# Merge in pieces, 512-column products, two sums by adding transfers and a rotary exchange on ScalarE in a decoder layer

## The chip, the cores and the metric

One core of one Trainium2 chip. TensorE (PE in the profile) multiplies, VectorE (DVE) and ScalarE (ACT) work on its results, GpSimd (POOL) and SyncE (SP) mostly issue transfers. The metric is the device time of one execution in microseconds; shorter is better.

## The reference

One layer of a hybrid decoder trunk, float32, 512 tokens, width 2048. A normalized input goes through one wide projection whose columns feed three attention branches and three gates; the branches are projected back, gated, summed, and projected once more.

```python
h = rms_norm(x, norm_in_g[layer])
proj = jnp.einsum('bsd,de->bse', h, w_in[layer])
(qa, ka, va, za, qb, kb, vb, zb, qm, zm, gates) = jnp.split(proj, split_points, axis=-1)
...
ya = moba_attention(qa, ka, va).reshape(B, S, W_A) * jax.nn.silu(za)
...
g_a, g_b, g_m = jnp.split(jax.nn.sigmoid(gates), N_BRANCH, axis=-1)
merged = (g_a * jnp.einsum('bse,ed->bsd', ya, w_proj_a[layer])
          + g_b * jnp.einsum('bse,ed->bsd', yb, w_proj_b[layer])
          + g_m * jnp.einsum('bse,ed->bsd', ym, w_proj_m[layer]))
x = x + jnp.einsum('bsd,de->bse', merged, w_out[layer])
return rms_norm(x, norm_final_g)
```

`qa`, `ka`, `qb` and `kb` are turned by rotary angles: with a head's 128 channels cut into halves x1 and x2, the result is x1 cos - x2 sin and x2 cos + x1 sin.

## The kernel before

Every float32 operand is split into a high part `hi` (a copy by ACT in the type fp32r) and a remainder `lo` (a difference by DVE), and a product is three products: hi x hi, hi x lo and lo x hi.

The wide projection is done in 65 *pairs* of output units of 128 channels (class `Pair`). Each pair is a 2 x 2 block product in seven block products instead of eight (a Strassen form): sums of weight quarters meet prepared forms of the activations, B11, T1, T2, B21, T3, B22 and T4, each 1024 x 256. B11, T4, B21 and B22 lie in the tiles `kept`, T1, T2 and T3 in tiles called `T`; each tile holds the high and the low part. One of the seven is `seven()`: for eight blocks of 128 rows it issues L397 (hi weights, high form), L398 (hi weights, low form) and L399 (lo weights, high form), 256 columns each, so a pair has 168 products. Three accumulators x, y and z in PSUM take them.

The weights of a pair come as quarters of 128 x 1024 (512 KB) by `quarter` (L378, on SP's queue): a11, a21, s (which is a22), a12, and a22 once more. They use 18 buffers `raw`, of which the forms T1 to T3 hold 12. `parts_1024` (L387 on ACT, L388 on DVE) splits one into `whi` and `wlo`, three buffers each. In the order of the seven products the split weights are p1 = a11; p5 = s after L435 (s = a21 + s); p6 = s after L441 (s = s + a11); p2 = a12; q7 = a21 after L448 (a21 = a21 + a11); q3 = s after L454 (s = s + a12); and p4 = a22. ACT copies x or y out at L443, L450 and L456; DVE forms the results g1 and g2 at L462, L468 and L474 from PSUM and these copies; ACT writes the last quarter, with sign and activation, at L481. L470 and L476 apply an activation (37 pairs have one for g2).

`Pair.run` emits a pair in seven steps, and after each it emits a share of a list `later` of small jobs, so that DVE's and ACT's side work lies among PE's products. The last step of a pair begins the next one (`follower`). The order on each engine is made by the planner of the Tile framework, from its own costs and what is ready; it is not the order of the text, so that L435 of the next pair, for example, stands ahead of L468 of this one. Each engine then works through its queue in order.

Turning (`rotate`): t1 = g cos, t2 = the exchanged halves of g times sin, L506 and L509, each on 64 partitions, then a sum; 40 times.

The last part before the output projection is the merge stage: eight times three pairs of gates (24 pairs). After each pair L1101 multiplies both results with the branch's projection `pj`, fetched from DRAM on POOL's queue, and L1103 adds them to `merged`; after three pairs `merged_forms` makes the activation forms for the output projection (five operations on DVE, L921 to L924 and the remainder of L927, one on ACT) and stores three tiles in DRAM (`waiting`). Then the output projection runs (L1038 to L1040), with final normalization.

Small tiles of 128 x 512 share 25 slots (`slot`). The code that the diff touches:

## Time and profile before

| what | value |
|---|---|
| three runs | 1997.02, 1999.28 and 2000.56 us, median 1999.28 us |
| the profiled execution | 2003.55 us, of which its span is 2001.8 us |
| PE, DVE, ACT, POOL busy | 98%, 76%, 51%, 6% of the span |
| matrix products, vector operations, activations | 14225, 1948, 1567 |
| bytes moved | 318.90 MB, 159 GB/s on average |
| loads of w_in of 512 KB | 331 issues |

The span runs from the first to the last instruction of one profiled execution. An engine's share is the time in which it had an instruction at work; a product of PE is longer in the profile than its distance to the next one, since products overlap, so products are told by distance here. Of a stage, the rows of a stretch tell more than the shares of the whole.

### The profile page before, as it was taken

What the parts mean: (1) busy time and instruction counts of PE and PEld (TensorE: products, weight loads), DVE (VectorE), ACT (ScalarE), POOL (GpSimd) and SP (SyncE); (2) the same over time, 40 slices, a digit from 0 to 9 for tenths busy, and PEclk for the clock granted to TensorE, in tenths of its full rate; (3) what the DMA queues carried; (4) which work ended last, traced back from release to release, by engine and by line L of the source; (5) the groups of instructions that cost most, each with busy time, mean ns of one, the idle gap of its engine ahead of it and who ended that gap; (6) DMA issues with size and microseconds to landing.
All of it is one profiled execution on the core that took longest, in us unless ns stands there. A gap on an engine that the chain in (4) does not pass through costs nothing.

```text
span 2001.8 us, 34970 instructions
## 1 busy us (share of the span) xinstructions
PE 1962.3 (98%) x14225; PEld 1850.3 (92%) x14225; DVE 1527.3 (76%) x1948; ACT 1019.9 (51%) x1567; POOL 118.4 (6%) x226
## 2 busy tenths in 40 slices
PE   8999999999999999999999999999999999999998
PEld 6889999789999999889999999989999999998776
DVE  5976777249999888348888889646878878778887
ACT  7654565245656665235545464644444444445445
POOL 0000010010000000010000000012000000001010
PEclk9999999999999999999999999999999999999999
DMA  9565444333333434433443434356445444558654
GB/s 364 189 222 172 149 159 156 134 112 132 127 122 126 128 118 157 142 132 117 122 138 106 134 115 127 117 174 205 140 163 181 161 155 143 180 171 302 251 181 152
DMA packets 100993, 318.90 MB, mean 159 GB/s; under 512 B 17376, under 2 KB 20320, under 8 KB 100832
## 3 DMA queue, kind: packets, MB, share of 16 engines
q1 hardware_dynamic: 84624, 264.21, 39.5%
q0 software_dynamic: 16064, 52.44, 7.7%
q8 instruction: 111, 1.82, 0.4%
q14 instruction: 50, 0.41, 0.1%
q10 hardware_dynamic: 144, 0.02, 0.0%
HBM read 285.13 MB, written 31.49 MB: 158 GB/s over the span
## 4 chain that ended last, share of the span: by engine, by line
PE 86%; DVE 5%; DMA 5%; issue 2%; ACT 1%; SPq 0%; ACTq 0%; DVEq 0%; POOL 0%; POOLq 0%
PE acc L397 19%; PE acc L398 19%; PE acc L399 19%; PE acc L112 5%; PE acc L110 5%; PE acc L111 5%; DMA raw<-in_w_in 2%; PE acc L1039 2%; PE acc L1040 2%; PE acc L1038 2%; DVE wlo L388 1%; DMA rows<-in_x 1%; PE att L162 1%; PE att L161 1%; PE att L163 1%
## 5 line engine op out<-in xcount | busy, mean ns | idle before, releaser
L387 ACT ACTIVATE whi<-raw 128x1024 fp32r<-128x1024 f32 x507 | 537.1, 1060 | 605.7 <-PE acc L398 359.6
L388 DVE TENSOR_TENSOR wlo<-raw,whi 128x1024 fp32r<-128x1024 f32 x507 | 617.7, 1220 | 137.5 <-ACT whi L387 125.8
L397 PE MATMUL acc<-kept,whi 128*128 128x256 f32 x2080 | 590.0, 284 | 13.7 <-DVE g L468 13.7
L398 PE MATMUL acc<-kept,whi 128*128 128x256 f32 x2080 | 586.8, 282 | 0.0
L399 PE MATMUL acc<-kept,wlo 128*128 128x256 f32 x2080 | 586.3, 282 | 0.0
L397 PE MATMUL acc<-T,whi 128*128 128x256 f32 x1560 | 441.6, 283 | 0.5 <-ACT ha L443 0.5
L399 PE MATMUL acc<-T,wlo 128*128 128x256 f32 x1560 | 441.0, 283 | 0.0
L398 PE MATMUL acc<-T,whi 128*128 128x256 f32 x1560 | 440.9, 283 | 0.0
L397 PEld LDWEIGHTS acc<-kept,whi 128*128 128x128 f32 x2080 | 394.3, 190 | 15.6 <-issue 14.7
L398 PEld LDWEIGHTS acc<-kept,whi 128*128 128x128 f32 x2080 | 394.7, 190 | 0.4
L399 PEld LDWEIGHTS acc<-kept,wlo 128*128 128x128 f32 x2080 | 394.8, 190 | 0.0
L397 PEld LDWEIGHTS acc<-T,whi 128*128 128x128 f32 x1560 | 297.8, 191 | 1.1 <-ACT ha L443 0.7
L399 PEld LDWEIGHTS acc<-T,wlo 128*128 128x128 f32 x1560 | 298.1, 191 | 0.4 <-DVE wlo L388 0.4
L398 PEld LDWEIGHTS acc<-T,whi 128*128 128x128 f32 x1560 | 298.2, 191 | 0.3
L91 DVE TENSOR_TENSOR wlo<-raw,whi 128x1024 fp32r<-128x1024 f32 x78 | 94.9, 1222 | 128.6 <-ACT whi L90 128.5
L90 ACT ACTIVATE whi<-raw 128x1024 fp32r<-128x1024 f32 x78 | 82.2, 1059 | 158.9 <-PE acc L111 105.7
L435 DVE TENSOR_TENSOR raw<-raw 128x1024 f32<-128x1024 f32 x65 | 79.5, 1223 | 89.9 <-DMA raw<-in_w_in 87.8
L110 PE MATMUL acc<-shi,whi 128*128 128x512 f32 x320 | 126.6, 396 | 0.5 <-ACT pr L145 0.5
L111 PE MATMUL acc<-slo,whi 128*128 128x512 f32 x320 | 126.5, 395 | 0.0
L112 PE MATMUL acc<-shi,wlo 128*128 128x512 f32 x320 | 126.4, 395 | 0.0
L441 DVE TENSOR_TENSOR raw<-raw 128x1024 f32<-128x1024 f32 x65 | 79.3, 1221 | 1.0
L454 DVE TENSOR_TENSOR raw<-raw 128x1024 f32<-128x1024 f32 x65 | 79.3, 1220 | 0.9
(268 smaller groups left out, 2585.3 us busy)
## 6 DMA issues: line engine op xcount, KB each, us to landing
raw<-in_w_in SPq DMA_DIRECT2D x331, 512.0 KB, 3.8
raw<-in_w_out SPq DMA_DIRECT2D x48, 512.0 KB, 6.6
raw<-in_w_mem SPq DMA_DIRECT2D x32, 512.0 KB, 5.2
projected<-pr POOLq DMA_DIRECT2D x48, 256.0 KB, 2.5
pj<-projected POOLq DMA_DIRECT2D x48, 256.0 KB, 5.6
raw<-in_w_pm SPq DMA_DIRECT2D x16, 512.0 KB, 3.8
raw<-in_w_pa SPq DMA_DIRECT2D x16, 512.0 KB, 4.2
mg<-waiting SPq DMA_DIRECT2D x9, 512.0 KB, 8.4
```

Of the source, the lines that this page charges most:

```text
L90: nc.scalar.activation(hi, raw, AF.Copy)
L91: nc.vector.tensor_tensor(lo, raw, hi.bitcast(F32), op=OP.subtract)
L110: nc.tensor.matmul(ps, whi, hi[i], start=i == 0, stop=False)
L111: nc.tensor.matmul(ps, whi, lo[i], start=False, stop=False)
L112: nc.tensor.matmul(ps, wlo, hi[i], start=False, stop=i == n - 1)
L387: nc.scalar.activation(hi, raw, AF.Copy)
L388: nc.vector.tensor_tensor(lo, raw, hi.bitcast(F32), op=OP.subtract)
L397: nc.tensor.matmul(ps, hi[:, sl], f[0], start=start and k == 0, stop=False, skip_group_check=True)
L398: nc.tensor.matmul(ps, hi[:, sl], f[1], start=False, stop=False, skip_group_check=True)
L399: nc.tensor.matmul(ps, lo[:, sl], f[0], start=False, stop=stop and k == 7, skip_group_check=True)
L435: nc.vector.tensor_tensor(s, a21, s, op=OP.add)
L441: nc.vector.tensor_tensor(s, s, a11, op=OP.add)
```

## The change

- `seven` issues two products per block instead of three: the hi weights meet the high and the low part of a form in one instruction of 512 columns, in two strips of 256 (the forms are views of both parts now), and the lo weights meet the high part, 256 columns, into the first half. The accumulators are 512 wide.
- The copies and sums out of PSUM are 512 wide (`both_tile`, three buffers), and `joined` adds the two halves of each on DVE. The last quarter is copied by ACT with its sign, added by DVE, and gets its activation apart.
- For pairs outside the memory branch (`adding`, 60 of 65) the sums L448 and L454 are made by transfers on POOL's queue that read the quarter a11 or a12 from DRAM again and add it to a21 or s in the buffer.
- `rotate` lets ACT copy the exchanged halves into t2, and DVE multiplies t2 by sin in one operation of 128 partitions. The table's signs are exchanged.
- The merge after each gate pair, and `merged_forms`, now cut into two, go into `later` and run beside the next pair, but for the last triple.
- `ones`, `diag`, `v` and the half tiles come from the slots; `v3` and `p` share a tag.

```diff
 
-    ones = sb.tile([P, P], F32, name="ones")
+    ones = slot("ones")[:, :P]
     nc.gpsimd.memset(ones, 1.0)
...
             for t in range(n):
-                diag = sb.tile([P, P], F32, name="diag", bufs=1)
+                diag = slot("diag")[:, :P]
                 nc.vector.tensor_scalar(diag, ident, col[:, t:t + 1], None, op0=OP.mult)
...
         b11, b12, b21, b22 = g0[:, :256], g0[:, 256:], g1[:, :256], g1[:, 256:]
-        u, v = slot("u"), sb.tile([P, 256], F32, name="halft", tag="halft", bufs=4)
+        u, v = slot("u"), slot("v")[:, :256]
         nc.vector.tensor_tensor(u[:, :256], b11, b12, op=OP.subtract)
...
         t = wide_tile("T12", F32R)
-        two = split(u, (t[:, :512], t[:, 512:]))
-        T["T1"].append([p[:, :256] for p in two])
-        T["T2"].append([p[:, 256:] for p in two])
+        split(u, (t[:, :512], t[:, 512:]))
+        two = t.rearrange("p (a c) -> p a c", a=2)
+        T["T1"].append(two[:, :, :256])
+        T["T2"].append(two[:, :, 256:])
         if k % 2 == 0:
...
         t = T["store"][:, k % 2 * 512:(k % 2 + 1) * 512]
-        T["T3"].append(split(v, (t[:, :256], t[:, 256:])))
+        split(v, (t[:, :256], t[:, 256:]))
+        T["T3"].append(t.rearrange("p (a c) -> p a c", a=2))
         split(g0, kept[k])
...
 
-    T["B11"] = [(t[:, 0, :256], t[:, 1, :256]) for t in held[:8]]
-    T["T4"] = [(t[:, 0, 256:], t[:, 1, 256:]) for t in held[:8]]
-    T["B21"] = [(t[:, 0, :256], t[:, 1, :256]) for t in held[8:]]
-    T["B22"] = [(t[:, 0, 256:], t[:, 1, 256:]) for t in held[8:]]
+    T["B11"] = [t[:, :, :256] for t in held[:8]]
+    T["T4"] = [t[:, :, 256:] for t in held[:8]]
+    T["B21"] = [t[:, :, :256] for t in held[8:]]
+    T["B22"] = [t[:, :, 256:] for t in held[8:]]
 
...
 
+    def add_quarter(t, u, half):
+        nc.gpsimd.dma_start(t, w_in[u][:, half * 1024:(half + 1) * 1024], accum_op=OP.add)
+    def both_tile(name):
+        return sb.tile([P, 512], F32, name=name, tag="both", bufs=3)
     def half_tile(name):
-        return sb.tile([P, 256], F32, name=name, tag="halft", bufs=4)
+        return slot(name)[:, :256]
+    def joined(out, t):
+        nc.vector.tensor_tensor(out, t[:, :256], t[:, 256:], op=OP.add)
 
...
 
         hi, lo = parts
...
             f = T[form][k]
-            nc.tensor.matmul(ps, hi[:, sl], f[0], start=start and k == 0, stop=False, skip_group_check=True)
-            nc.tensor.matmul(ps, hi[:, sl], f[1], start=False, stop=False, skip_group_check=True)
-            nc.tensor.matmul(ps, lo[:, sl], f[0], start=False, stop=stop and k == 7, skip_group_check=True)
+            nc.tensor.matmul(ps, hi[:, sl], f, start=start and k == 0, stop=False, skip_group_check=True)
+            nc.tensor.matmul(ps[:, :256], lo[:, sl], f[:, 0, :], start=False, stop=stop and k == 7,
+                             skip_group_check=True)
 
...
         def __init__(self, u1, u2, f1=AF.Copy, f2=AF.Copy):
+            self.adding = u1 < U_QM or u1 >= U_G
             self.units, self.f1, self.f2 = (u1, u2), f1, f2
...
             a12 = quarter(u1, 1)
             p5 = parts_1024(s)
-            x = acc_bank()[:, :256]
+            x = acc_bank()
             seven(x, p1, "B11", start=True)
             nc.vector.tensor_tensor(s, s, a11, op=OP.add)
-            a = half_tile("ha")
+            a = both_tile("ha")
             nc.scalar.copy(a, x)
             yield 1
             p6 = parts_1024(s)
-            y = acc_bank()[:, :256]
+            y = acc_bank()
             seven(y, p5, "T1", start=True)
-            nc.vector.tensor_tensor(a21, a21, a11, op=OP.add)
-            d = half_tile("hd")
+            if self.adding:
+                add_quarter(a21, u1, 0)
+            else:
+                nc.vector.tensor_tensor(a21, a21, a11, op=OP.add)
+            d = both_tile("hd")
             nc.scalar.copy(d, y)
             yield 2
             p2 = parts_1024(a12)
             seven(x, p6, "T2")
-            nc.vector.tensor_tensor(s, s, a12, op=OP.add)
-            b = half_tile("hb")
+            if self.adding:
+                add_quarter(s, u1, 1)
+            else:
+                nc.vector.tensor_tensor(s, s, a12, op=OP.add)
+            b = both_tile("hb")
             nc.scalar.copy(b, x)
             yield 3
             q7 = parts_1024(a21)
-            z = acc_bank()[:, :256]
+            z = acc_bank()
             seven(z, p2, "B21", start=True, stop=True)
             g1 = self.g1 = slot("g1")
-            nc.vector.tensor_tensor(g1[:, :256], z, a, op=OP.add)
+            nc.vector.tensor_tensor(a, z, a, op=OP.add)
+            joined(g1[:, :256], a)
             yield 4
             q3 = parts_1024(s)
...
             seven(x, q7, "T3")
             g2 = self.g2 = slot("g2")
-            nc.vector.scalar_tensor_tensor(g2[:, 256:], x, -1.0, d, op0=OP.mult, op1=OP.subtract)
+            nc.vector.scalar_tensor_tensor(d, x, -1.0, d, op0=OP.mult, op1=OP.subtract)
+            joined(g2[:, 256:], d)
             if self.f2 != AF.Copy:
                 nc.scalar.activation(g2[:, 256:], g2[:, 256:], self.f2)
...
             p4 = parts_1024(a22)
             seven(y, q3, "B22", stop=True)
-            nc.vector.tensor_tensor(g1[:, 256:], y, b, op=OP.add)
+            nc.vector.tensor_tensor(b, y, b, op=OP.add)
+            joined(g1[:, 256:], b)
             if self.f1 != AF.Copy:
                 nc.scalar.activation(g1, g1, self.f1)
...
                 self.follower.begin()
             seven(x, p4, "T4", stop=True)
-            nc.scalar.activation(g2[:, :256], x, self.f2, scale=-1.0)
+            e = both_tile("he")[:, :256]
+            nc.scalar.activation(e, x[:, 256:], AF.Copy, scale=-1.0)
+            nc.vector.scalar_tensor_tensor(g2[:, :256], x[:, :256], -1.0, e, op0=OP.mult, op1=OP.add)
+            if self.f2 != AF.Copy:
+                nc.scalar.activation(g2[:, :256], g2[:, :256], self.f2)
             yield 7
 
...
         def first():
+            nc.scalar.copy(t2[0:64], g[64:128])
+            nc.scalar.copy(t2[64:128], g[0:64])
             nc.vector.tensor_tensor(t1, g, cos, op=OP.mult)
-            nc.vector.tensor_tensor(t2[0:64], g[64:128], sin[64:128], op=OP.mult)
 
         def second():
-            nc.vector.tensor_tensor(t2[64:128], g[0:64], sin[0:64], op=OP.mult)
+            nc.vector.tensor_tensor(t2, t2, sin, op=OP.mult)
             r = t1
...
     M = {f: [None] * 8 for f in ("T1", "T2", "T3")}
-    M.update({f: T[f] for f in ("B11", "T4", "B21", "B22")})
+    M.update({f: [(t[:, 0], t[:, 1]) for t in T[f]] for f in ("B11", "T4", "B21", "B22")})
     waiting = dram.tile([NK, P, 512], F32, name="waiting")
...
     def merged_forms(k):
         g0, g1 = merged[k], merged[8 + k]
...
         u, v = slot("u"), half_tile("v")
-        nc.vector.tensor_tensor(u[:, :256], b11, b12, op=OP.subtract)
-        nc.vector.tensor_tensor(v, b22, b12, op=OP.subtract)
-        nc.vector.scalar_tensor_tensor(u[:, 256:], u[:, :256], -1.0, b22, op0=OP.mult, op1=OP.subtract)
-        nc.vector.scalar_tensor_tensor(b12, u[:, 256:], -1.0, b21, op0=OP.mult, op1=OP.subtract)
-        for at, t in ((waiting[k], g0), (waiting[8 + k], g1), (waiting3[k // 4][:, k % 4 * 256:(k % 4 + 1) * 256], v)):
-            nc.gpsimd.dma_start(at, t)
-        two = split(u)
-        M["T1"][k] = [p[:, :256] for p in two]
-        M["T2"][k] = [p[:, 256:] for p in two]
+        def first():
+            nc.vector.tensor_tensor(u[:, :256], b11, b12, op=OP.subtract)
+            nc.vector.scalar_tensor_tensor(u[:, 256:], u[:, :256], -1.0, b22, op0=OP.mult, op1=OP.subtract)
+            two = split(u)
+            M["T1"][k] = [p[:, :256] for p in two]
+            M["T2"][k] = [p[:, 256:] for p in two]
+        def second():
+            nc.vector.tensor_tensor(v, b22, b12, op=OP.subtract)
+            nc.vector.scalar_tensor_tensor(b12, u[:, 256:], -1.0, b21, op0=OP.mult, op1=OP.subtract)
+            for at, t in ((waiting[k], g0), (waiting[8 + k], g1),
+                          (waiting3[k // 4][:, k % 4 * 256:(k % 4 + 1) * 256], v)):
+                nc.gpsimd.dma_start(at, t)
+        return first, second
+    def merge(dt, g, pr):
+        nc.vector.tensor_tensor(g, g, pr, op=OP.mult)
+        if merged[dt] is None:
+            merged[dt] = g
+        else:
+            nc.vector.tensor_tensor(merged[dt], merged[dt], g, op=OP.add)
 
...
             done.run()
-            for dt, g, pr in zip(pair, (done.g1, done.g2), prs):
-                nc.vector.tensor_tensor(g, g, pr, op=OP.mult)
-                if n:
-                    nc.vector.tensor_tensor(merged[dt], merged[dt], g, op=OP.add)
-                else:
-                    merged[dt] = g
+            later.extend([lambda a=a: merge(*a) for a in zip(pair, (done.g1, done.g2), prs)])
         if i == 7:
+            flush()
             split(merged[7][:, :256], M["B11"][7])
-        merged_forms(i)
+            for f in merged_forms(7):
+                f()
+        else:
+            later.extend([lambda i=i: pieces_of.append(merged_forms(i)),
+                          lambda: pieces_of[-1][0](), lambda: pieces_of[-1][1]()])
 
```

## Rows read from the trace of the kernel before

**Rows 1.** The cores: span in us, mean granted clock of TensorE.

```profile
core 0: 2001.8 us, clock 0.994
```

**Rows 2.** The page, part 1: busy us, share of the span, instructions.

```profile
PE 1962.3 (98%) x14225; PEld 1850.3 (92%) x14225; DVE 1527.3 (76%) x1948; ACT 1019.9 (51%) x1567; POOL 118.4 (6%) x226
```

**Rows 3.** Stretches: length, then busy us by engine, granted clock, DMA share, GB/s.

```profile
991.70:1051.63 59.93, 59.93 (x506) 59.93 (x505) 52.60 (x58) 27.36 (x35) 0.56 (x1) 1.00 0.43 137
1385.49:1784.69 399.20, 385.75 (x3194) 384.53 (x3193) 318.66 (x367) 183.89 (x254) 34.22 (x63) 0.99 0.49 165
43.80:76.40 32.60, 32.60 (x141) 26.07 (x140) 30.88 (x59) 23.91 (x42) 2.85 (x5) 1.00 0.73 276
500.00:600.00 100.00, 100.00 (x829) 99.48 (x829) 90.24 (x122) 58.97 (x97) 1.62 (x3) 1.00 0.38 123
```

**Rows 4.** Waits of PE, 1380 to 1830: us in total, times, longest.

```profile
PE acc L397 <- DVE g L468: 13.4, 7, 2.8
```

**Rows 5.** The chain that ended last, 1395 to 1412: start, us, what.

```profile
1394.06 5.57 DMA raw<-in_w_in
```

**Rows 6.** Timeline of DVE: start, us, line, operation, tiles, idle before.

```profile
1399.72 1.23 DVE L435 TENSOR_TENSOR raw<-raw 128x1024 f32<-128x1024 f32 x1 [3.20 <-DMA raw<-in_w_in]
...
1403.47 0.41 DVE L468 SCALAR_TENSOR_TENSOR g<-acc,hd 128x256 f32<-128x256 f32 x1
...
1429.47 1.23 DVE L388 TENSOR_TENSOR wlo<-raw,whi 128x1024 fp32r<-128x1024 f32 x1
```

**Rows 7.** Waits of the load queue, 1380 to 1830.

```profile
SPq L378 <- DVE raw L454: 76.8, 13, 6.8
```

**Rows 8.** Timeline of PE.

```profile
1441.22 0.28 PE L397 MATMUL acc<-kept,whi 128*128 128x256 f32 x1
...
1885.40 0.39 PE L1040 MATMUL acc<-whi,T 128*128 128x512 f32 x1
...
1887.89 0.39 PE L1039 MATMUL acc<-wlo,T 128*128 128x512 f32 x1
```

**Rows 9.** Groups by line: count | busy us, mean ns | idle before.

```profile
L454 DVE TENSOR_TENSOR raw<-raw 128x1024 f32<-128x1024 f32 x65 | 79.3, 1220 | 0.9
...
L145 ACT ACTIVATE pr<-acc 128x512 f32<-128x512 f32 x48 | 27.8, 586 | 12.8 <-PE acc L112 11.9 <-PE att L162 0.9
...
L509 DVE TENSOR_TENSOR t<-g,sin 64x512 f32<-64x512 f32 x40 | 27.4, 685 | 0.8
...
L462 DVE TENSOR_TENSOR g<-acc,ha 128x256 f32<-128x256 f32 x65 | 27.0, 416 | 1.3 <-PE acc L399 1.3
...
L481 ACT ACTIVATE g<-acc 128x256 f32<-128x256 f32 x65 | 24.7, 380 | 78.4 <-PE acc L399 78.4
...
L110 PE MATMUL acc<-kept,whi 128*128 128x512 f32 x48 | 19.0, 396 | 0.0
...
L1049 DVE TENSOR_TENSOR res<-res,acc 128x512 f32<-128x512 f32 x24 | 15.7, 679 | 3.9 <-PE acc L1040 3.1 <-DMA res<-in_x 0.8
...
L470 ACT ACTIVATE g<-g 128x256 f32<-128x256 f32 x37 | 15.3, 414 | 30.2 <-DVE g L468 30.1
```

**Rows 10.** Timeline of ACT.

```profile
1428.38 1.06 ACT L387 ACTIVATE whi<-raw 128x1024 fp32r<-128x1024 f32 x1 [0.86 <-DVE raw L441]
...
1435.64 1.06 ACT L387 ACTIVATE whi<-raw 128x1024 fp32r<-128x1024 f32 x1 [1.55 <-issue]
```

**Rows 11.** DMA: queue q1 (packets, MB, share); issues, KB each, us to landing.

```profile
q1 hardware_dynamic: 84624, 264.21, 39.5%
...
raw<-in_w_in SPq DMA_DIRECT2D x331, 512.0 KB, 3.8
...
mg<-waiting SPq DMA_DIRECT2D x9, 512.0 KB, 8.4
...
yf<-ydram POOLq DMA_DIRECT2D x14, 256.0 KB, 3.3
```

More of the change, by code (lines that the diff above doesn't have):

```diff
@@ L545, in third @@
     def third(h):
-        return sb.tile([P, P], F32, name="v3", bufs=2)
+        return sb.tile([P, P], F32, name="v3", tag="tail", bufs=2)
     ydram = dram.tile([16, P, 512], F32, name="ydram")
@@ L732, in transposed @@
             else:
-                p = sb.tile([P, P], F32, name="p", bufs=2)
+                p = sb.tile([P, P], F32, name="p", tag="tail", bufs=2)
                 nc.scalar.copy(p, tp[:, at])
@@ L1084, in early_sum @@
         nc.vector.tensor_scalar(early[:, t:t + 1], early[:, t:t + 1], 1.0 / D, EPS, op0=OP.mult, op1=OP.add)
+    pieces_of = []
     for i in range(8):
@@ L1218, in _rope @@
     return np.ascontiguousarray(
-        np.stack([np.concatenate([cos, cos]), np.concatenate([sin, -sin])], axis=1).astype(np.float32))
+        np.stack([np.concatenate([cos, cos]), np.concatenate([-sin, sin])], axis=1).astype(np.float32))
 def kernel(**inputs):
```

## The prediction, made before the changed kernel had run

> **What bounds the kernel now.** I read the share of busy time first: PE 98%, DVE 76%, ACT 51% [rows 2]. An average says little, so I cut out one stretch of pure pair work and the whole merge stage [rows 3]. Three pairs from 991.70 hold 504 products of 256 columns in 59.93 us at a granted clock of 1.00 (two that began before are counted in the row): 118.9 ns from one to the next, 168 of them make 19.98 us for a pair, and PE never idles. 65 pairs make 65 x 19.98 = 1298 us of the 2001.8 us span [rows 1]. So in pair work only what shortens PE's own stream counts; DVE and ACT matter only where they make PE wait.
>
> The merge stage is different. From 1385.49 to 1784.69 run 19 pairs; at 19.98 us they would take 379.6 us, they take 399.2: 19.6 us lost [rows 3]. The waits of PE name it: seven times, 13.4 us in all, the first product of a pair waits for DVE's L468 [rows 4]. The clock in the row is 0.99, not 1.00; the other 6 us are mostly that. Follow one such wait back: a load issued at 1394.06 landed 5.57 us later [rows 5]; DVE's L435, the sum of two loads for the *next* pair, idled DVE 3.20 us for it and ran at 1399.72, and L468, queued behind it, ran at 1403.47 [rows 6]. Why was the load late? Loads wait for DVE to finish with a buffer, 76.8 us in this stage for L454 alone [rows 7]. DVE releases late because at the end of every third pair four multiply-adds and the whole of the merged forms come on it together.
>
> **The change, part by part.**
>
> *512 columns in one product.* Of the three products per weight block, two become one of 512 columns, the third stays: 65 x 7 x 8 = 3640 times, 2 x 118.9 = 237.8 ns become the price of one 512. Pair work has no such product. The nearest are L110 to L112 early on, the same `kept` tiles moving past `whi` weights, 512 columns [rows 9]: from 43.80 to 76.40, 32.60 us for some 140, 233 ns [rows 3]. Saved: 4.8 ns x 3640 = 17.5 us. The quickest stretch of them has 226 ns (1885.40 to 1887.89, eleven steps, with other weights) [rows 8]: then 41 us. The other end is 237.8, nothing saved, since the moving operand now comes in two strips. I take 233. The 256-column remainder I leave at 118.9.
>
> The Trainium skill ("TensorE: Matmul & The Clock Gate", Back-to-back issue gap) gives a product N/2.4 + 2.5 ns; one instruction less would then save 2.5 ns, 9 us in all, and the result would be 1975, inside the forecast's own range below. The rows differ: 256 columns take 118.9 here, not 109, and 512 take 233, not 216.
>
> *Evictions and the joining sums.* Three 256-column evictions on DVE of 0.42 us (L462 stands for them) become 512 wide, as L1049, 0.68; three joins of 256 columns come, 0.42 each, and the last eviction becomes ACT's copy `e` (0.38, as L481) and a DVE operation of 0.42 [rows 9]. DVE: +3 x 0.26 + 3 x 0.42 + 0.42 = +2.5 us per pair. Where two of the 1.22-us sums (L448, L454) go to transfers, 2.4 us go too: DVE stays level. Five memory pairs keep them and get 2.5 us more, under PE. ACT: three copies of 256 columns (0.38 at most, as L481) become 512 wide (0.59, as L145), and 37 pairs get the activation of one quarter apart (0.41, as L470): 3 x 0.21 + 0.41 = 1.0 us per pair of 20. ACT is idle half of the time, so I cost it at nothing; without that cover it would be 65 x 1.0 = 65 us. At the end of a pair the chain is longer by some 0.5 to 1 us (copy, operation, activation instead of one activation). Queued behind it on DVE is the next pair's L441, for which ACT's split waits [rows 10]; the removed sums leave DVE room to run L441 before it. I count 0, at most 65 x 0.5 = 33 us.
>
> *Rotary halves.* 40 times DVE loses one half-height product, 0.69 us as the remaining one (L509), and ACT gets two half-height copies of at most 0.59 us each (as L145) [rows 9]: DVE -27 us, ACT +47 us. Both lie under PE (attention stretch 500 to 600: PE 100%, DVE 90%, ACT 59% [rows 3]). Zero.
>
> *Merge in pieces.* The merges and forms keep their operations; they are spread over the next pair's steps. The burst that made the loads late goes, and the adding transfers free two load buffers earlier: a12 after its split instead of after L454, a11 after L441. So L435 gets its operands 1 to 3 us sooner. I take 17 of the 19.6 us, the rest staying as one wait or so; ends 0 and 19.6.
>
> *The adding transfers.* Sixty pairs issue two each on POOL's queue: 120 of 512 KB. Price in transfer time: a plain 512 KB occupies all 16 engines for 0.395 x 2001.8 us x 0.524 / 264.21 = 1.57 us [rows 11]; adding must read the destination too, so an estimate of 3.1 us, 6.3 us per pair. The transfer engines stand at 38 to 49% [rows 3]; with 6.3 of 20 us more, 70 to 81%. Enough, if an add costs no more than two copies.
>
> Latency matters more. The first add (into a21) can start right after L435, about 10 us before its pair begins, and is split some 6 us into it: harmless. The second (into s) is tight. Take the pair that begins at 1426.93. The split at 1428.38 waits for L441, so it is p6, and its DVE half ends at 1430.7; from there the transfer may start. The third split after it, 1435.64, is q3, the reader of s; its product starts at 1441.22 [rows 6, 8, 10]. Split on ACT 1.06, on DVE 1.22, minus 0.23 since the second half is needed one product later: ACT must start by 1439.1. So s has 5.0 us before anything moves and 8.4 us before PE waits. What will it take? A plain load of this size lands in 3.8 us on SP's queue, a POOL transfer of half the size in 3.3 [rows 11]; half the size more is 0.8, the second read 1.57: 5.7 us, my estimate. Lower end 3.8; upper end the 8.4 of the 512 KB loads from `waiting` plus 1.57: 10 us. I take 5.7: no wait of PE. What is late then is only ACT's split by 0.7 us, with nothing urgent behind it.
>
> The Trainium skill speaks against this part ("Collectives: The Full Stack", The bandwidth ceiling): a reducing transfer reads two sources and gets half the rate. No run so far shows it; by that an add has the same 3.1 us that I use.
>
> POOL's queue: the adds stand among `pj` fetches, `ydram` and `waiting` stores, in the planner's order, which rows of before don't show. A store that waits for DVE holds up the adds behind it. I put 2 us on this, and on slots: `ones`, `diag`, `v` and the half tiles now share the 25 slots.
>
> Sum: -17.5 - 17 + 2 = -32.5 us. The profiled execution took 2003.55, so 1971; the median of the runs is 4.3 us lower, so **1967 us**.
>
> **The rivals.**
> 1. *The add into s lands late* (slower). POOL's issue, two reads and SP's loads on the same engines. From 8.4 us on every microsecond costs up to 60: at 9.0 the whole gain is gone, at 10 us 96 us are lost, less 32.5: 2063 us. For it: nothing in this trace adds in flight, and the longest landing of this size is 8.4. Against it: loads of this size land in 3.8.
> 2. *One gain is missing.* The 512 costs as two 256: -17 + 2, 1984. Or the adds crowd the loads so that L435 keeps waiting in the merge stage: -17.5 + 2, 1984. For it: transfers there reach 49%, and landing was 5.57 when it mattered.
> 3. *Larger gain*: 226 ns and all of the merge stage: -41 - 19.6, 1939.
> 4. *Nothing comes of it*: waits of 0.5 us per pair at the pair's end eat the gain: -32.5 + 33, 2000.
>
> **How the numbers follow.** Forecast 0.55 (1955 to 1983), one gain missing 0.15, late adds 0.19, larger gain 0.06, nothing 0.05. A measurement here can tell 0.2%, 4 us. Faster 0.76, same 0.05, slower 0.19. The range 1945 to 2005 leaves out the larger gain (0.06) and most of the late adds (0.14).
>
> **What would show it.** Right: pair stretches of 112 products in about 19.7 us; no wait of PE for L468's successor in the merge stage; adds landing in about 6 us; DVE level. Wrong: ACT's or DVE's split of s waiting for a transfer, and PE behind it at the sixth group of products of a pair; the 512 at 238 ns; POOL's adds issued long after L435; L435 waiting longer than now.

## The result: 2.7% slower, and the profile after

The changed kernel takes 2052.72 us (median of 4 runs, 2052.0 to 2057.38) against 1999.7 us, ratio 1.0272 (95%: 1.0254 to 1.0291). The forecast was 1967.

The page of the changed kernel (part 1: busy us, share, instructions; then one queue, one group, two kinds of transfer with KB each and us to landing):

```profile
PE 1967.9 (96%) x10585; PEld 1673.5 (82%) x10585; DVE 1497.6 (73%) x2048; ACT 1116.5 (54%) x1684; POOL 222.5 (11%) x346
...
q0 software_dynamic: 33344, 115.36, 27.0%
...
L448 DVE TENSOR_TENSOR raw<-raw 128x1024 f32<-128x1024 f32 x65 | 79.6, 1224 | 165.7 <-DMA raw<-in_w_in 156.9
...
raw<-in_w_in SPq DMA_DIRECT2D x331, 512.0 KB, 5.2
raw<-in_w_in POOLq DMA_DIRECT2D x120, 512.0 KB, 6.0
```

3640 products fewer, and PE has fallen from 98% to 96% [rows 2]. The adding transfers land in 6.0 us; plain loads need 5.2 in place of 3.8 [rows 11]. The waits over the whole span (us in total, times, longest):

```profile
ACT whi L398 <- DMA raw<-in_w_in: 160.0, 49, 5.7
DVE raw L448 <- DMA raw<-in_w_in: 156.9, 48, 4.9
...
PE acc L409 <- ACT hb L475: 40.5, 36, 2.5
```

The wait of [rows 4] (L468, now L488) is gone, and a new one stands in its place: PE waits for the copy `hb`, and ACT's split for a transfer. (Lines have moved: L435 is now L448, L441 L454, L456 L475, L387/L388 L398/L399, L397/L398 L409, L399 L410; the old L448 and L454 are both the adding L384.) The last 22 gate pairs as one stretch:

```profile
1387.39:1866.89 479.50, 451.15 (x2465) 384.93 (x2464) 364.69 (x469) 235.25 (x323) 76.14 (x112) 0.98 0.75 208
```

21.8 us for a pair, at a transfer share of 0.75 in place of 0.49 [rows 3]. One of these pairs, from its first product at 1737.69, in the timeline (start, us, engine, line; in brackets the idle time before, and what ended it):

```profile
1740.73 1.23 DVE L399 TENSOR_TENSOR wlo<-raw,whi 128x1024 fp32r<-128x1024 f32 x1 [0.25 <-ACT whi L398]
...
1742.26 0.89 POOL L384 DMA_DIRECT2D raw<-in_w_in  x1 [9.57 <-DVE wlo L399]
...
1744.40 0.56 ACT L466 COPY hd<-acc 128x512 f32<-128x512 f32 x1
1748.11 1.06 ACT L398 ACTIVATE whi<-raw 128x1024 fp32r<-128x1024 f32 x1 [3.15 <-DMA raw<-in_w_in]
1749.08 0.57 ACT L475 COPY hb<-acc 128x512 f32<-128x512 f32 x1
...
1749.70 0.50 PE L409 MATMUL acc<-T,whi 128*128 128x512 f32 x1 [0.65 <-ACT hb L475]
...
1749.83 1.23 DVE L448 TENSOR_TENSOR raw<-raw 128x1024 f32<-128x1024 f32 x1 [4.07 <-DMA raw<-in_w_in]
```

p6's DVE half ends at 1741.96, the transfer into s is issued at once, q3's split begins at its landing, 1748.11, 5.85 us later. Behind it in ACT's queue stands `hb`, and for `hb` PE waits. DVE's L448, for the next pair, has idled 4.07 us for a load by then. The pair lasts 20.97 us, a clean one 19.63.

Where the time went, by stretches: from the first products of pairs 1, 8, 24 and 44 (from there the last 22 pairs, all gates) to the first product after the pairs, in the profiled execution. Lengths of before in us, of the others the difference to it. The profiled execution of before was one of its slower ones (2003.55 us), so a row's differences add up to some 2 to 10 us less than its ratio says. Each ratio is against before on the same chip; e3, e4 and e6 ran once and have no interval. Medians of different chips differ by some us, so small differences between kernels are better read from the ratios.

| kernel | median us | ratio [95%] | to pair 1 | 1-7 | 8-23 | 24-43 | 44-65 | after |
|---|---|---|---|---|---|---|---|---|
| before | 1999.7 | 1 | 170.1 | 262.3 | 449.8 | 483.4 | 459.1 | 177.1 |
| changed | 2052.7 | 1.0272 [1.0254, 1.0291] | -0.2 | +1.2 | -0.7 | +21.5 | +20.4 | +5.9 |
| e1 no transfer | 1984.9 | 0.9943 [0.9927, 0.9958] | -1.0 | -1.0 | +0.1 | +1.6 | -19.0 | +0.5 |
| e2 first only | 1973.7 | 0.9888 [0.9869, 0.9908] | +0.2 | -1.9 | -4.1 | -4.4 | -26.1 | +5.5 |
| e3 second only | 2113.1 | 1.059 | -0.5 | -0.2 | +19.7 | +39.4 | +42.2 | +8.3 |
| e4 hb on VectorE | 2047.3 | 1.026 | -1.3 | -1.9 | +3.2 | +26.9 | +10.8 | +6.0 |
| e5 aside, loose | 2095.4 | 1.0495 [1.0472, 1.0518] | +118.3 | -1.5 | -3.9 | -3.1 | -25.8 | +7.0 |
| e6 17 buffers | 2088.5 | 1.046 | +0.4 | +8.2 | +26.7 | +17.7 | +27.5 | +4.4 |
| e7 rotary as before | 1981.8 | 0.9921 [0.9894, 0.9947] | +0.1 | -0.5 | -1.3 | +0.4 | -25.7 | +6.9 |
| e8 merge as before | 1968.7 | 0.9858 [0.9838, 0.9879] | -0.8 | -0.8 | -4.1 | -3.2 | -26.3 | +1.1 |
| e9 aside, in place | 1996.5 | 0.9980 [0.9968, 0.9992] | -0.1 | +7.5 | -2.9 | +3.6 | -22.5 | +8.5 |
| e10 512 columns only | 2021.7 | 1.0107 [1.0081, 1.0132] | -0.4 | +1.6 | +14.9 | +13.2 | -13.9 | +1.9 |
| e11 first in all pairs | 1973.6 | 0.9875 [0.9859, 0.9892] | -1.2 | +1.2 | -4.1 | -1.2 | -26.4 | +1.7 |
| e12 second on GpSimd | 2028.9 | 1.0149 [1.0128, 1.0170] | -1.0 | +0.0 | -1.3 | +17.0 | +8.9 | +1.2 |
| e13 tiny transfer | 2079.4 | 1.0405 [1.0377, 1.0433] | -0.6 | +3.8 | +0.1 | +11.6 | +54.4 | +1.2 |

### The profile page after: what moved, and what is told of

Read it like the earlier page. It is cut to its first block, busy times and chain, and to the rows that moved or that the text cites. A ratio compares the mean times of both kernels' runs of the same rounds, so it can differ in the third digit from the quotient of the medians.

```text
span 2049.9 us, 28128 instructions
## 1 busy us (share of the span) xinstructions
PE 1967.9 (96%) x10585; PEld 1673.5 (82%) x10585; DVE 1497.6 (73%) x2048; ACT 1116.5 (54%) x1684; POOL 222.5 (11%) x346
## 4 chain that ended last, share of the span: by engine, by line
PE 40%; issue 21%; DVE 19%; DMA 15%; ACT 3%; POOL 1%; DVEq 0%; ACTq 0%; SPq 0%; POOLq 0%
PE acc L409 14%; DMA raw<-in_w_in 12%; DVE wlo L399 9%; PE acc L410 7%; PE acc L110 3%; PE acc L111 3%; PE acc L112 3%; DVE raw L454 1%; ACT whi L398 1%; PE acc L1081 1%; PE acc L1082 1%; PE acc L1080 1%; DVE ha L481 1%; DVE hd L488 1%; DVE g L393 1%
## 5 line engine op out<-in xcount | busy, mean ns | idle before, releaser
L398 ACT ACTIVATE whi<-raw 128x1024 fp32r<-128x1024 f32 x507 | 535.2, 1060 | 540.0 <-PE acc L409 175.8
L409 PE MATMUL acc<-kept,whi 128*128 128x512 f32 x2080 | 746.1, 399 | 5.7 <-ACT whi L398 1.8
L399 DVE TENSOR_TENSOR wlo<-raw,whi 128x1024 fp32r<-128x1024 f32 x507 | 616.8, 1221 | 160.2 <-ACT whi L398 154.1
L409 PE MATMUL acc<-T,whi 128*128 128x512 f32 x1560 | 567.2, 403 | 42.1 <-ACT hb L475 40.5
L410 PE MATMUL acc<-kept,wlo 128*128 128x256 f32 x2080 | 586.8, 282 | 1.8 <-DVE wlo L399 1.7
L409 PEld LDWEIGHTS acc<-kept,whi 128*128 128x128 f32 x2080 | 391.8, 188 | 101.4 <-issue 5.3
L410 PE MATMUL acc<-T,wlo 128*128 128x256 f32 x1560 | 443.5, 284 | 1.9 <-DVE wlo L399 1.9
L409 PEld LDWEIGHTS acc<-T,whi 128*128 128x128 f32 x1560 | 297.1, 190 | 123.4 <-ACT hb L475 54.4
L410 PEld LDWEIGHTS acc<-kept,wlo 128*128 128x128 f32 x2080 | 394.1, 189 | 4.1 <-DVE wlo L399 3.5
L410 PEld LDWEIGHTS acc<-T,wlo 128*128 128x128 f32 x1560 | 299.3, 192 | 4.8 <-DVE wlo L399 4.4
L384 POOL DMA_DIRECT2D raw<-in_w_in x120 | 104.7, 872 | 1034.9 <-DVE raw L448 445.0
L448 DVE TENSOR_TENSOR raw<-raw 128x1024 f32<-128x1024 f32 x65 | 79.6, 1224 | 165.7 <-DMA raw<-in_w_in 156.9
L454 DVE TENSOR_TENSOR raw<-raw 128x1024 f32<-128x1024 f32 x65 | 79.4, 1221 | 0.6
L110 PEld LDWEIGHTS acc<-shi,whi 128*128 128x128 f32 x320 | 60.0, 188 | 15.4 <-ACT pr L145 0.9
L112 PEld LDWEIGHTS acc<-shi,wlo 128*128 128x128 f32 x320 | 60.0, 188 | 14.6
L111 PEld LDWEIGHTS acc<-slo,whi 128*128 128x128 f32 x320 | 60.1, 188 | 14.4
L495 DVE TENSOR_TENSOR hb<-acc,hb 128x512 f32<-128x512 f32 x65 | 44.7, 688 | 10.6 <-PE acc L410 10.6
```

The lines of the kernel that those rows point to most:

```text
L110: nc.tensor.matmul(ps, whi, hi[i], start=i == 0, stop=False)
L111: nc.tensor.matmul(ps, whi, lo[i], start=False, stop=False)
L112: nc.tensor.matmul(ps, wlo, hi[i], start=False, stop=i == n - 1)
L384: nc.gpsimd.dma_start(t, w_in[u][:, half * 1024:(half + 1) * 1024], accum_op=OP.add)
L398: nc.scalar.activation(hi, raw, AF.Copy)
L399: nc.vector.tensor_tensor(lo, raw, hi.bitcast(F32), op=OP.subtract)
```

## The experiments

**Which transfer costs.** One or both sums go back to VectorE (e1 both; e2 the second; e3 the first). The edit of e2:

```diff
-            if self.adding:
-                add_quarter(s, u1, 1)
-            else:
-                nc.vector.tensor_tensor(s, s, a12, op=OP.add)
+            nc.vector.tensor_tensor(s, s, a12, op=OP.add)
```

What was expected of e1, e2 and e3, in this order:

> All sums on VectorE, no adding transfer; every other part of the change stays. Theory T (the second adding transfer, into s, lands late, ScalarE's split q3 waits for it, and the copy hb queued behind that split holds up the product T3): the wait of PE for hb, 40 us, is gone, and the time falls below before, to about 1965 us; VectorE then carries 2.5 us more per pair and may be full in the attention part, so less than the 1953 that the products alone would give. Rival C (120 more transfers crowd the loads, so that the sum of the next pair's loads, L448, waits): the same, about 1965. Rival X (the wide evictions, the longer end of a pair, the exchange on ScalarE or the merge in pieces cost the time): stays near 2045 us.

> Only the sum into a21 is an adding transfer, 60 of them; the sum into s is VectorE's again. T: nothing waits for an adding transfer, about 1960 us, and the wait of PE for hb is under 5 us. C: half of the extra traffic stays, and with it half of the loss against no adding transfer, about 2005 us, with VectorE's L448 waiting some 120 us for loads. X: about 2045 us.

> Only the sum into s is an adding transfer. T: nearly the whole loss stays, 2035 to 2055 us, with 30 to 40 us of PE waiting for hb. C: half of the loss, about 2005 us. X: about 2045 us.

The first transfer alone is worth 11 us (e1 to e2), the second costs 79 (e2 to the changed kernel; 77 by the ratios). e3 moves as many bytes as e2 and ends 139 us later, so bytes alone explain little. PE waits 42.7 us for `hb` in e3, as the theory has it, and not at all in e2; but its times were missed, by 20 us in e1, 14 in e2 and 58 in e3, all upwards. Two stretches of e2, three clean pairs and the 22 gate pairs:

```profile
1474.33:1533.21 58.88, 58.88 (x338) 51.48 (x337) 52.73 (x67) 32.20 (x43) 7.61 (x12) 1.00 0.67 196
...
1355.34:1788.36 433.02, 432.63 (x2466) 377.51 (x2464) 388.93 (x491) 238.78 (x323) 56.45 (x90) 1.00 0.69 205
```

58.88 / 3 = 19.63 us for a pair, and 22 x 19.63 = 431.9 of 433.0: nothing is lost there any more, at a transfer share of 0.69.

**Is it ACT's order?** `hb` goes to VectorE, so that it no longer stands behind q3's split.

```diff
-            nc.scalar.copy(b, x)
+            nc.vector.tensor_copy(b, x)
```

> Both adding transfers stay, but the copy hb out of PSUM is VectorE's, so that it no longer stands behind ScalarE's split of s; in about half of the pairs the planner puts it behind L448 on VectorE instead, which waits for loads. T: PE's wait in front of T3 goes in the pairs where hb stands ahead of L448; the time falls by 15 to 40 us, to about 2020. C: unchanged, 2050 us.

Only 5 us better in all (2 by the ratios, from a single run), against the 15 to 40 expected: 9.6 in the gates, lost again in pairs 8 to 43. A gate pair of e4 (start 1735.48) shows the next one in line, DVE's timeline:

```profile
1748.06 1.23 DVE L448 TENSOR_TENSOR raw<-raw 128x1024 f32<-128x1024 f32 x1 [3.30 <-DMA raw<-in_w_in]
1749.20 1.22 DVE L399 TENSOR_TENSOR wlo<-raw,whi 128x1024 fp32r<-128x1024 f32 x1
```

q3's DVE half is now behind a sum for the next pair whose load is late, and PE waits 0.62 us inside q3's product. So the order on ACT is where the lateness shows first; with `hb` out of the way, the next in line, a load that is late, holds up PE.

**Do buffers carry it on?**

```diff
-RAWS = 18
+RAWS = 17
```

> The changed kernel with 17 in place of 18 buffers of 512 KB (12 are held by the forms, so 5 in place of 6 for quarters). Theory that the lateness goes round by the buffers (s held longer, so the next loads start later): a pair needs its buffers longer than it lasts, one less of six costs up to a sixth of a 20 us pair where it binds, so 40 to 130 us more in the two query stages and the gates: 2090 to 2180 us, the waits of loads for buffers more than doubled. Rival (only ScalarE's order, q3's split ahead of hb, costs): within 10 us of 2052.

36 us more than the changed kernel in a single run, just under the range given and far above the rival's 10. But the loads' waits for buffers did not double: the largest, for DVE's splits, went from 567 to 604 us. And pairs 24 to 43 got 3.8 us shorter and the gates 7.1 longer: a buffer less costs in pairs 1 to 23 (+7.0, +27.4), hardly where the changed kernel loses. So buffers matter, but this run doesn't show that the changed kernel's lateness goes round by them.

**Traffic or dependence?** e2, and each second transfer issued all the same, into scratch memory that nothing reads. e5 left it loose; e9 ties it to its pair by a small store. The edit of e9 against e2 (e5 is without the first of the two transfers):

```diff
...
             nc.vector.tensor_tensor(s, s, a12, op=OP.add)
+            if self.adding:
+                nc.gpsimd.dma_start(aside[u1 % 8][:, :16], s[:, :16])
+                nc.gpsimd.dma_start(aside[u1 % 8], w_in[u1][:, 1024:2048], accum_op=OP.add)
```

Expected of e5, then of e9:

> The first sum by transfer, the second on VectorE as in e2_first_only, and beside it every second transfer is issued all the same at its place in GpSimd's order, but into scratch memory that nothing reads. The traffic, the issues and the queue are those of the changed kernel; nobody waits for the second transfer. Theory (the way through s is too long: q3's split waits for the landing, s's buffer comes free late): the time of e2_first_only within 0.4%, ratio 0.986 to 0.993 to the kernel before, no waits of PE for hb, although queue 0 holds some 27% again. Rival (27% on queue 0 slows loads and the queue): 2035 to 2055 us, ratio 1.02 to 1.03, loads landing in 5.2 us or more and L448's wait for loads again above 100 us.

> e5_add_aside again, with the transfers kept at their place: its 60 transfers into scratch hung on nothing and ran in the first 250 us, ahead of the pairs, so it did not put the traffic beside the products. Here each is preceded by a small store (16 columns) of the finished s into the same scratch, so it can start only when its pair has its second sum. Theory (what costs is that q3 waits for the landing and that s is held): stages from the memory pairs to the gates as in e2_first_only within 8 us in sum, 1970 to 1985 us, loads landing near 4.5 us. Rival (traffic and the queue cost): the query stage B and the gates each 15 us or more longer than in e2_first_only, 2025 to 2055 us.

e5 says nothing on the question: all 60 transfers ran in the first 250 us, where the 118 us were lost. In e9 they are in their places:

```profile
q0 software_dynamic: 35264, 115.86, 26.0%
```

With nearly the share of the changed kernel it takes 23 us more than e2 (18 by the ratios), between the theory's 0 to 11 and the rival's 51 to 81; no wait for `hb` returns. So traffic takes some 18 to 23 of the 77 to 79 us, and this is probably too much: these transfers write to DRAM, which the change doesn't do, the adds into a21 land in 9.4 us in place of e2's 6.9, and 9.4 of the 23 us are lost in pairs 1 to 7, where the changed kernel is only 3.1 slower than e2.

e13 is the reverse: the sum on VectorE, and behind it 16 of the 1024 columns added once more by a transfer. Its edit against e2:

```diff
             nc.vector.tensor_tensor(s, s, a12, op=OP.add)
+            if self.adding:
+                nc.gpsimd.dma_start(s[:, :16], w_in[u1][:, 1024:1040], accum_op=OP.add)
```

> e2_first_only, its second sum on VectorE, and behind it a transfer that adds 16 of the 1024 columns again (so these columns get the quarter twice): 8 KB in place of 512 KB, at the place of the changed kernel's second transfer. The wait of q3's split for a landing is back, the traffic is not. Theory (dependence costs some 56 of the 79 us between e2_first_only and the changed kernel, traffic the 23 that e9_aside_tied shows): the landing of a tiny transfer takes 2 to 3 us, with 0.9 of issue and the sum's 1.2 in front 4 to 5 us in place of 7, so a part of the 56 us: 1985 to 2030 us, PE waiting for hb again in the gates. Rival (traffic costs it all): within 0.4% of e2_first_only, 1966 to 1982 us, no waits for hb.

106 us more than e2, with 0.5 MB more moved. So a wait for a landing costs this much with next to no traffic, more than the changed kernel loses. The number was missed upwards, since the landing was mis-estimated: median 4.4 us, and in the gates more, as ACT's timeline shows (one gate pair; POOL issued at 1713.24):

```profile
1713.39 0.59 ACT L474 COPY hb<-acc 128x512 f32<-128x512 f32 x1 [1.72 <-PE acc L410]
1720.31 2.95 ACT L398 ACTIVATE whi<-raw 128x1024 fp32r<-128x1024 f32 x3 [6.34 <-DMA raw<-in_w_in]
```

```profile
PE acc L409 <- ACT whi L398: 31.9, 25, 3.6
PE acc L410 <- DVE wlo L399: 22.4, 35, 0.8
```

Here the planner put `hb` ahead of the split, against what was expected, and PE waits for q3's two halves themselves (waits over the span). The way is also longer than the changed kernel's: the sum on DVE comes first, and in this pair q3's split starts 9.9 us after p6's half, against 6.15 in the pair shown above. So e13 shows that the wait alone can cost this much, not how much of the changed kernel's loss it is; for that the 56 us that e9 leaves over (59 by the ratios) are the measure.

**A third latency.** e8 (merge as before, see below) with the second sum on GpSimd.

```diff
-            nc.vector.tensor_tensor(s, s, a12, op=OP.add)
+            eng = nc.gpsimd if self.adding else nc.vector
+            eng.tensor_tensor(s, s, a12, op=OP.add)
```

> e8_merge_before with the second sum by GpSimd's own add (after the same wait, no transfer). No traffic is added, VectorE is as free as in the changed kernel; only the time that the sum takes differs, which no row shows: from VectorE's 1.2 us up. Theory (what counts is when s is ready for q3's split, 8 us after p6's VectorE half at the latest minus what stands behind the split): if GpSimd's add ends within 3 us, the time is that of e8_merge_before or up to 6 us better, 1962 to 1970 us, the two query stages 2 to 6 us shorter. If it takes 5 us or more, the stages lose as with the transfer, 1990 to 2030 us. Rival (VectorE no longer limits once the first sum has gone): 1967 to 1971 us whatever the sum takes below 5 us.

The add takes 2.72 us, under the 3 that was to be harmless, and the kernel is 60 us slower than e8: a miss. Timelines of POOL (first line) and DVE, one gate pair:

```profile
1597.43 2.72 POOL L471 TENSOR_TENSOR raw<-raw 128x1024 f32<-128x1024 f32 x1 [10.93 <-DVE wlo L399]
...
1597.81 3.43 DVE L399 TENSOR_TENSOR wlo<-raw,whi 128x1024 fp32r<-128x1024 f32 x1
```

A split that takes DVE 1.22 us lasted 3.43: it ended 1.1 us after GpSimd's add did, so it ran behind it, not beside it. 38 of the 60 adds met a split that took 3.3 to 3.5 us; in e8 none takes over 1.23. DVE is busy 1596 us against e8's 1562, with 60 sums fewer. And ACT's splits waited for the sum on GpSimd only 1.5 us in all, so this run doesn't measure latency: what costs here is DVE held up.

**The other parts.** e7 undoes the rotary exchange in e2, e8 the merge in pieces; e10 has the 512-column products with their evictions and joins, and both sums, the merge and the rotary exchange as before; e11 is e8 with the first transfer in the five memory pairs too. The edits of e7 (first half) and e8 (in part) against e2:

```diff
-            nc.scalar.copy(t2[0:64], g[64:128])
-            nc.scalar.copy(t2[64:128], g[0:64])
             nc.vector.tensor_tensor(t1, g, cos, op=OP.mult)
+            nc.vector.tensor_tensor(t2[0:64], g[64:128], sin[64:128], op=OP.mult)
...
```

> e2_first_only with the rotary halves exchanged by VectorE's products as in the kernel before: VectorE gets back 40 half-height products of 0.69 us (27 us), ScalarE loses 80 copies. Prediction's term, zero: ratio to e2 within 0.2%, so 1970 to 1978 us. Rival (VectorE is what the two query stages wait for once the products are shorter, as e1_no_add shows, where shorter products brought nothing there): 5 to 20 us more, all between the memory pairs and the end of the query stages, 1979 to 1994 us.

```diff
-            later.extend([lambda a=a: merge(*a) for a in zip(pair, (done.g1, done.g2), prs)])
+            for dt, g, pr in zip(pair, (done.g1, done.g2), prs):
+                nc.vector.tensor_tensor(g, g, pr, op=OP.mult)
...
```

Expected of e8, then of e10:

> e2_first_only with the merge in one go as in the kernel before. Prediction's term (17 of the 19.6 us lost in the merge come back by the pieces): some 17 us more than e2_first_only, 1988 to 1994 us, all of it in the gates' stage. Rival (the merge was hidden or the gain there came from shorter products): 1972 to 1979 us.

> Only the products of 512 columns with their evictions and joins; both sums, the merge and the rotary halves as in the kernel before. The clean pair is 0.35 us shorter. Prediction's term: 17.5 us faster, 1977 to 1983 us, spread over all stages by their pairs. Rival (VectorE, with 2.5 us more for each pair, is what the query stages and the merge wait for): nothing in the two query stages, and in the merge nothing or a loss, 1992 to 2005 us. By e1_no_add and e8_merge_before the gates tell whether the merge's 19 us come back by pieces or by the sum that is taken off VectorE: if the gates here gain 15 us or more, the shorter products alone do it; if they gain under 5, either cure is needed.

The edit of e11 against e8:

```diff
-            self.adding = u1 < U_QM or u1 >= U_G
+            self.adding = True
```

> e8_merge_before with the first sum by transfer in the memory pairs too (5 pairs more). Theory (VectorE is short wherever pairs run beside attention, the first transfer has 10 us of room): 1965 to 1969 us, the memory stage 1 to 2 us shorter. Rival (another 5 transfers change nothing or come late): 1968 to 1975 us.

e7: the exchange is worth 9 us in pairs 1 to 43, 7 to 8 in all; its interval and e2's touch. e8: the pieces bring nothing to the gates (432.8 and 433.0 us) and lose 4.4 us after them. e11 brings nothing. e10 is the surprise: the shorter products, with the evictions that they need and nothing else, make the kernel 21 us slower. The pairs 8 to 23 of e10 and of e8:

```profile
433.60:898.30 464.70, 454.17 (x2458) 383.70 (x2457) 382.75 (x533) 252.49 (x402) 16.24 (x30) 1.00 0.40 125
```

```profile
430.80:876.50 445.70, 444.91 (x2458) 384.07 (x2457) 353.01 (x499) 277.10 (x438) 30.36 (x46) 1.00 0.52 149
```

DVE, the fourth number behind the window, is busy 382.75 us of 464.70 in e10, and PE idles 10.5; with one half-height rotary product and the first sum off it, it is 353.01, and PE idles 0.8. By the page's chain of work that ended last, e10 hangs on DVE as much as on PE, e8 on PE (first line e10, second e8):

```profile
PE 21%; DVE 21%; DMA 7%; issue 5%; ACT 1%; POOL 0%; SPq 0%; DVEq 0%; ACTq 0%; POOLq 0%
```

```profile
PE 80%; issue 11%; DVE 4%; DMA 3%; ACT 1%; POOL 0%; SPq 0%; ACTq 0%; POOLq 0%; DVEq 0%
```

The fastest is e8, 1968.7 us, 1.4% faster than before: 512 columns, first sum by transfer, rotary on ScalarE, merge as it was.

## Why the prediction was wrong

**The step that failed** is the last sentence on latency: "no wait of PE. What is late then is only ACT's split by 0.7 us, with nothing urgent behind it". The landing itself was well sized: 5.7 us estimated, 6.0 measured, and 5.85 from the issue to q3's split in the pair shown. The deadline was wrong, in two ways.

First, it was reckoned from q3's own product, the sixth of the pair: 8.4 us of room. But in ACT's queue the next instruction behind q3's split is `hb`, which the *fifth* product needs. With 19.63 / 7 = 2.80 us for a product that one is due 11.2 us after the pair's start; with 1.06 for the split and 0.57 for the copy ahead of it (they overlap by 0.1) the split must start at 9.7. From 4.3, where p6's half ended in the pair shown, that leaves 5.4 us, the shortest landing of all 120 adds (5.4 to 9.3), and 0.3 of issue comes on top. The split began at 10.4, 0.7 us late, and PE waited 0.65; over the span it waited 36 times for `hb`, 40.5 us. The same order, a split between `hd` and `hb`, stood in ACT's queue before the change; I read the timeline as far as the split [rows 10] and not one row on:

```profile
1436.61 0.35 ACT L456 COPY hb<-acc 128x256 f32<-128x256 f32 x1
```

The fifth product of that pair began at 1438.36, so by this row s had 1438.36 - 0.35 - 0.97 - 1430.7 = 6.3 us, and an estimated 5.9 once the copy is wider and the products are shorter. Against a landing estimated at 5.7 that is no room, where 8.4 looked safe.

Second, the lateness doesn't end with the pair. e4 takes `hb` out and wins at most 5 us, since then q3's DVE half, queued behind a sum that waits for its load, is late. That each pair's late s makes the next pair's loads late is what these rows suggest, but it is not shown; e6 shows that buffers matter, but not mainly where the change loses. How the 56 us that traffic doesn't explain divide between the two ways is open. Waits are not the whole loss either: the 22 gate pairs take 46.5 us more than in e2, of which PE's listed waits are 28.2 (22.1 for `hb`). By the granted clock, 0.98 in place of 1.00, an estimated 10 us more are lost (0.02 x 479.5); the rest is not assigned.

**The rivals.** Rival 1, the late add, is what happened, but at a landing of 6.0 us and not from 8.4 on. By its own price it would have cost nothing at 6.0, and only one of the 120 adds took longer than 8.4; its chance of 0.19 came from the wrong deadline. So the direction of the rival came true, not its reckoning. Its 8.4 for the longest landing of this size was misread: that is the median of the loads from `waiting`, which took up to 13.3 us, and loads of `w_in` took up to 9.0.

**512 columns, -17.5 us.** On PE the term was too small: a clean pair is 19.63 us against 19.98, so 65 x 0.35 = 23 us were there, inside the bounds. But with the evictions that they need, e10 shows +21.

**Evictions and joins, 0.** They are the likely reason. DVE's extra time, 2.5 us for a pair (162 in 65), was counted level with the two sums; the page of e10 has DVE busy 1650.5 us, 123 more than before [rows 2]. Taken by itself this is not hidden: pairs 8 to 43 lose 28 us in e10, and taking other work off DVE wins them back (e1, e8). Whether the longer chain at the end of a pair, put at 0 to 33 us, has a part in it was not tried apart.

**Rotary, 0.** In e2 the exchange is worth 9 us in pairs 1 to 43, and between e10 and e1, where both sums are still on DVE, pairs 1 to 43 gain 29.0, ahead of nearly all of the merge. A busy share of 90% in a stretch [rows 3] was read as cover; it was where the next microsecond of DVE would be paid for.

**Merge in pieces, -17.** The loss of 19.6 us was real and it went, but by e8 without the pieces: 432.8 us for 22 pairs are 1 us over 22 clean ones. Step by step the gates give 13.9 (e10), of which 7.7 are the shorter products, 5.1 more with the pieces (e10 to e1), 7.1 more with the first transfer (e1 to e2). The burst was taken for the only cause; one sum less on DVE does as much without the pieces (e8), and then they have nothing left to do. Why 6 us went already in e10, where DVE has more work, stays open.

**Transfers' price, 3.1 us.** (0.270 x 2049.9 - 0.077 x 2001.8) / 120 = 3.3 us of 16 engines for an add, 0.077 being the share of the same queue before; against 1.57 us for a plain load this is 2.1 times. By the Trainium skill ("Collectives: The Full Stack", The bandwidth ceiling) a reducing transfer reads two sources at half the rate; this case agrees. The price was right, but its cost in time, 18 to 23 us by e9, was put at 0 in the sum.

**POOL's queue, +2.** The term was not measured apart; the issue in the pair shown came 0.3 us after p6's half. The stretch after the pairs is 4 to 9 us longer only in kernels with both pieces and transfers, though not in e13; why was not tried.

The parts in order, on the ratios times 2000 us: 512 columns with evictions +21 (e10); rotary and pieces -33 (e10 to e1); the first transfer -11 (e1 to e2); the second +77 (e2 to the changed kernel); together +54. Each holds for this order: on top of the other parts the pieces cost 5 to 6 us (e8 to e2).

## What to carry to other kernels

Before a sum is moved from an engine to a transfer, count its room not to the product that reads it, but to the earliest use of anything queued behind the waiting instruction on its engine; one more row of the timeline would have shown some 6 us of room in place of 8.4. Two edits of the same kind can have opposite signs: the first transfer has some 14 us of room (issued at 1751.35 for the split at 1765.02 in the changed kernel) and paid 11 us, the second has 5.4 and cost 77. So try them apart. And where an engine is 80 to 90% busy beside a full PE, as DVE is in e10, time given to it or taken from it is not free.

## What the runs showed of the hardware

A transfer that adds 8 KB lands not much sooner than one of 512 KB; from e13, its landing:

```profile
DMA to landing us min/median/max: 2.2/4.4/7.5
```

against 5.4/6.0/9.3 for the 120 of 512 KB in the changed kernel: a sixty-fourth of the bytes takes about a quarter off the median. GpSimd spent 0.87 us on issuing either.

GpSimd's add and DVE's split, both with two operands in SBUF, ran one after the other (e12, above). The Trainium skill ("SBUF — State Buffer", SBUF: two separate sides) has GpSimd and a DVE operation with two SBUF inputs share one pair of ports by an exclusive lock; the rows agree: 1597.43 + 2.72 + 1.22 = 1601.37, and the split ended at 1601.24.

A wait of PE can cost twice, but need not. After 1.89 us of waiting for `hb` up to 1578.04 in the changed kernel the granted clock of the next stretch, up to 1582.30, was 0.60, between the levels of 1.2 and 2.4 GHz; after 2.10 us of waiting up to 1708.65 it was 1.00 (windows: length, busy us by engine, clock, transfer share, GB/s):

```profile
1578.04:1582.30 4.26, 4.26 (x15) 3.68 (x16) 3.94 (x5) 0.91 (x1) 1.87 (x3) 0.60 0.47 142
1708.65:1712.65 4.00, 4.00 (x23) 3.50 (x24) 4.00 (x6) 1.89 (x2) 1.83 (x3) 1.00 0.49 140
```

The product of a pair that began at 1578.04 took 4.46 us, to 1582.50, in place of 2.78 (1740.52 to 1743.30, at a clock of 1.00). What decides between the two cases these rows don't show.
